# Gate products by token tile instead of a seven-product scheme, and another order of the last products of a down-projection, in a two-layer decoder trunk

## The chip, the cores and the metric

The kernel runs on one core of one Trainium2 chip. The metric is the device time of one execution in microseconds (us). Engines are named as in the profile: PE multiplies matrices, PEld loads its weights, DVE is the vector engine, ACT the scalar engine, POOL the general one, SP issues most of the DMAs.

## The reference

512 tokens, width 1024, two layers, all in float32. Layer 0 mixes tokens by an mLSTM, layer 1 by sliding-window attention over a shared K/V that is computed after layer 0. Each layer ends in the same way, and only this end bears on the change:

```python
x = layer_norm(ALPHA * x + mix, mix_ln_g[i], mix_ln_b[i])
x = layer_norm(ALPHA * x + squared_relu_mlp(x, w_up[i], w_down[i]), mlp_ln_g[i], mlp_ln_b[i])
x = x + sigmoid(x @ w_gate[i] + b_gate[i]) * (p[i] @ w_proj[i])
```

`w_up` is 1024x4096, `w_down` 4096x1024, `w_gate` 1024x1024, `w_proj` 256x1024; `p[i]` is the embedding of the layer, 512x256. Below, "gate" means `x @ w_gate` with what follows it, and "embedding projection" `p @ w_proj`.

## The kernel before

**Number format.** Every float32 operand of a product is split into a high part (ACT, line 76, 133 or 546) and a low part (DVE, line 77, 134 or 547), and a product is three matmuls: high x high, low x high, high x low (`mm3`, lines 88, 89, 90). One "product of 24 matmuls" below is 8 blocks of 128x128 by 512 columns, three matmuls each.

**Tiles of tokens.** The residual is four tiles `res[0..3]` of 128 tokens by 1024. `XH`, `XL` hold the transposed activations, 8 blocks of 128 by 512 tokens, high and low.

**Weights.** `load_w` loads 128x1024 of a weight into `wraw` (three buffers), and splits it into `whi` and `wlo` (six buffers each). SP issues these loads.

**The seven-product scheme (`seven`).** A 512x1024 by 1024x1024 product is done as the seven half-size products M1 to M7 of the Strassen-Winograd scheme, in place of eight. It needs sums of weight blocks (lines 519, 522, 525, 529, on DVE, two each), sums of activation blocks (`S1`, `S23`, `S4A`), and a callback `on` that adds each product into the results it belongs to. The order is M1, M2, M5, M6, M7, M3, M4. The down-projection of an MLP is done so in four quarters of 1024 of the hidden width (`mlp`, q = 0..3), and the gate once per layer (`ple`).

**End of an MLP.** In the last quarter, M3 completes the residual of tiles 0 and 1 and M4 that of tiles 2 and 3. Each is followed by `ln_finish`: statistics (line 142), a power on POOL (138), two passes of DVE over 128x1024 (145, 146), and then `put_seven`, which transposes the tile on PE (565) and writes `XH`/`XL` for tiles 0 and 1, and, once the second of a pair (0,2), (1,3) is there, the activation sums for the gate. The layer norm's gain and bias are loaded by POOL into the two buffers `bc` after M7 has let go of them (lines 670 to 677).

**End of a layer (`ple`).** The embedding projection (16 groups of 3 matmuls; `p` lies in columns of `XH`/`XL` that are not in use) is written before the gate, so its 48 matmuls run right after M4. Then come the seven gate products; as each result is complete, sigmoid (ACT, 723), product with the projection (DVE, 724), addition to the residual (DVE, 725). In layer 0 `done` then transposes the tile (129) into `XH`/`XL` for the K/V projection that follows, whose weights are split on POOL (line 77 with engine POOL) rather than on DVE. In layer 1 the result goes to the output.

**What sets the order.** A list scheduler of the framework orders each engine's instructions once, when the kernel is built, by program order among those that its own estimate says are ready; on the chip each engine runs its list strictly in that order. Each tile is a fixed stretch of on-chip memory, and a tile may be written when the tiles that lay in that stretch before are released. A pool's tiles lie in the order of their first use. `pm` (of `mlp`, tiles `A11h`, `A11l`, `A12h`, `A12l`, `s1`) and `pp` (of `ple`) take turns on one stack: in layer 0 they end at the same byte (145376), in layer 1 they begin at the same byte (184320, where `A11h` lies).

Of the kernel before, what the change touches and what calls it, by code (L numbers as in the profile page):

```python
# [10 lines left out]
F32 = mybir.dt.float32  # L11
# [34 lines left out]
def yoco_kernel(ctx: ExitStack, tc: tile.TileContext, A: dict, out: bass.AP):  # L46
# [90 lines left out]
        V.tensor_scalar(dst, var, EPS, None, ALU.add)  # L137
        GP.tensor_tensor(dst, dst, nhalf[:, :n], ALU.pow)

    def ln_finish(t, st, g, b, put=None):  # L140
        mv = small.tile([P, 2], F32, tag="mv", name="mv")
        V.bn_aggr(mv, st)
        rs = small.tile([P, 1], F32, tag="rs", name="rs")
        rsqrt_eps(rs, mv[:, 1:2], 1)
        V.scalar_tensor_tensor(res[t], res[t], mv[:, 0:1], g, ALU.subtract, ALU.mult)
        V.scalar_tensor_tensor(res[t], res[t], rs, b, ALU.mult, ALU.add)  # L146
        if put is None:
            transpose_in(res[t], t, XH, XL)
            ACT.mul(res[t], res[t], ALPHA)
            if t >= 2:  # L150
                r = res[t - 2][:, 512:]
                V.tensor_sub(r, r, res[t][:, 512:])
        else:
            put(t)

    def add_res(t, half, ps, alpha):
        r = res[t][:, half * 512:(half + 1) * 512]
# [333 lines left out]
    def seven(A_, wsrc, on):  # L491
# [31 lines left out]
        product("S2", ops(r11), "M6")  # L523
        for c in range(2):
            V.tensor_add(r12[c], r12[c], r22[c])
        product("S3", ops(r12), "M7")
        product("S4", ops(r22), "M3")
        for c in range(2):
            V.tensor_add(r21[c], r21[c], r11[c])
        product("A22", ops(r21), "M4")  # L530
# [25 lines left out]
    half0 = {}  # L556

    def put_seven(t):

        a = t % 2  # L560
        raws = []
        for b in range(2):
            pt = tp_bank()
            for j in range(4):
                PE.transpose(pt[:, tsl(j)], res[t][:, tsl(4 * b + j)], ident)
            raw = xr()
            ACT.copy(raw, pt)
            raws.append(raw)
            if t < 2:
                v = raw.rearrange("p (k c) -> p k c", c=P)  # L570
                both_parts((XH[:, 4 * b:4 * b + 4, tsl(t)], XL[:, 4 * b:4 * b + 4, tsl(t)]), v)
        if t < 2:
            half0[t] = raws
            return
        a11, a12 = half0[a]
        a21, a22 = raws
        s1 = xr()
        V.tensor_sub(s1, a21, a22)
        V.tensor_sub(a21, a21, a11)
        V.tensor_sub(a11, a11, s1)  # L580
        V.tensor_sub(a12, a12, a11)
        sl = tsl(a)
        kc = lambda x: x.rearrange("p (k c) -> p k c", c=P)
        both_parts([x[:, :, sl] for x in sp["S1"]], kc(s1))
        both_parts([x[:, 0, :, sl] for x in sp["S23"]], kc(a11))
        both_parts([x[:, 1, :, sl] for x in sp["S23"]], kc(a21))
        both_parts([x[:, 0, :, sl] for x in sp["S4A"]], kc(a12))
        both_parts([x[:, 1, :, sl] for x in sp["S4A"]], kc(a22))

    def mlp(i, side):  # L590
        mctx = ExitStack()
# [5 lines left out]
        for q in range(NQ):  # L597
# [54 lines left out]
            def on(step, a, bank):  # L652
                r0, r1 = res[a], res[2 + a]
                t1, t6, t7 = T1[:, a, :], T6[:, a, :], T7[:, a, :]
                if step == "M1":
                    gather(t1, bank)
                    if last:
                        V.tensor_add(r0[:, lo_], r0[:, lo_], t1)
                elif step == "M2":
                    V.tensor_add(r0[:, lo_], r0[:, lo_], bank)  # L660
                    if last:
                        V.bn_stats(sts[a][:, 0, :], r0[:, lo_])
                elif step == "M5":
                    V.tensor_add(r1[:, hi_], r1[:, hi_], bank)
                    if last:
                        V.tensor_add(r0[:, hi_], r0[:, hi_], r1[:, hi_])
                elif step == "M6":
                    gather(t6, bank)
                    if last:
                        V.tensor_sub(t6, t6, t1)  # L670
                        V.tensor_add(r0[:, hi_], r0[:, hi_], t6)
                elif step == "M7":
                    gather(t7, bank)
                    if last:
                        V.tensor_add(t7, t7, t6)  # L675
                        V.tensor_add(r1[:, hi_], r1[:, hi_], t7)
                        V.tensor_sub(r1[:, lo_], r1[:, lo_], t7)
                        V.bn_stats(sts[2 + a][:, 1, :], r1[:, hi_])
                        if a == 1:
                            gb_[:] = [bcast(A["mlp_ln_g"][i]), bcast(A["mlp_ln_b"][i])]  # L680
                elif step == "M3":
                    V.tensor_add(r0[:, hi_], r0[:, hi_], bank)
                    if last:
                        V.bn_stats(sts[a][:, 1, :], r0[:, hi_])
                        ln_finish(a, sts[a], *gb_, put_seven)
                elif step == "M4":
                    V.tensor_add(r1[:, lo_], r1[:, lo_], bank)
                    if last:
                        V.bn_stats(sts[2 + a][:, 0, :], r1[:, lo_])
                        ln_finish(2 + a, sts[2 + a], *gb_, put_seven)  # L690
# [5 lines left out]
    def ple(i, last, side):  # L696
        plctx = ExitStack()
        pp = pool(f"pp{i}", stack=plctx, side=side, reuse_waits="tile")
        T = sp["T"]
        halves = (slice(0, 512), slice(512, 1024))  # L700
        raw = wpool.tile([P, 1024], F32, tag="raw", name="wraw", bufs=3)
        nc.sync.dma_start(raw, A["pT"][i])
        spare = [x[:, 0:4, 256:512] for x in (XH, XL)]
        both_parts(spare, raw.rearrange("p (j c) -> p j c", c=256))
        bg = bcast(A["ple_b_gate"][i])
        bs = pp.tile([P, 512], F32, name="bs")
        V.tensor_add(bs, bg[:, halves[0]], bg[:, halves[1]])
        pjs = {}
        for half in range(2):
            wph, wpl = load_w(A["w_proj"][i, half], 1024)  # L710
            for t in range(NT):
                pj = mm_bank()
                for k in range(2):
                    j = k * NT + t
                    h, l = (x[:, j // 2, (j % 2) * P:(j % 2 + 1) * P] for x in spare)
                    sl = slice(k * 512, (k + 1) * 512)
                    mm3(pj, h, l, wph[:, sl], wpl[:, sl], k == 0, k == 1)
                pjs[t, half] = pp.tile([P, 512], F32, name=f"pj{t}{half}")
                ACT.copy(pjs[t, half], pj)

        def fin(t, half, s, pj):
            r = res[t][:, halves[half]]
            ACT.activation(s, s, AF.Sigmoid)
            V.tensor_mul(s, s, pj)  # L724
            V.tensor_add(r, r, s)  # L725
            if last:
                nc.sync.dma_start(out[tsl(t), halves[half]], r)

        def stile():
            return xr()  # L730

        keep = {}

        def on(step, a, bank):
            if step == "M1":
                V.tensor_add(T[:, a, :], bank, bg[:, halves[0]])
            elif step == "M2":
                s = stile()
                V.tensor_add(s, T[:, a, :], bank)
                fin(a, 0, s, pjs[a, 0])  # L740
            elif step == "M5":
                s = keep["z", a] = stile()
                V.tensor_add(s, bank, bs)
            elif step == "M6":
                V.tensor_sub(T[:, a, :], bank, T[:, a, :])
                s = keep["c", a] = stile()
                V.tensor_add(s, T[:, a, :], keep["z", a])
            elif step == "M7":
                V.tensor_add(T[:, a, :], T[:, a, :], bank)
                s = keep["z", a]  # L750
                V.tensor_add(s, s, T[:, a, :])
                fin(2 + a, 1, s, pjs[2 + a, 1])
            elif step == "M3":
                s = keep["c", a]
                V.tensor_add(s, s, bank)
                fin(a, 1, s, pjs[a, 1])
                done(a)
            elif step == "M4":
                s = stile()
                V.tensor_sub(s, bank, T[:, a, :])  # L760
                fin(2 + a, 0, s, pjs[2 + a, 0])
                done(2 + a)

        if not last:
            bo = bcast(A["b_b_o"])

        def done(t):
            if last:
                return
            transpose_in(res[t], t, XH, XL)  # L770
            V.scalar_tensor_tensor(res[t], res[t], ALPHA, bo, ALU.mult, ALU.add)
            nc.sync.dma_start(spill[t], res[t])

        at = lambda b: lambda k, a: tuple(p[:, 4 * b + k, tsl(a)] for p in (XH, XL))
        seven(sset((at(0), at(1))), lambda half: [A["w_gate"][i, half, c] for c in range(4)], on)
        plctx.close()

    dpool = ctx.enter_context(tc.tile_pool(name="dpool", bufs=1, space=bass.MemoryType.DRAM))
# [290 lines left out]
```

## Time and profile before

| | |
|---|---|
| median of 3 runs | 1255.28 us (1254.99 to 1256.64) |
| the profiled execution's own time | 1252.41 us |
| its span in the profile | 1250.7 us |
| granted clock of PE, mean | 0.98 |
| PE busy | 1180.0 us, 94% |
| DVE busy | 932.4 us, 75% |
| ACT busy | 612.5 us, 49% |
| POOL busy | 150.2 us, 12% |

Times below are counted from the start of the span. The table of stretches (windows) in the profile gives, for each stretch, the busy time and the count of instructions of each engine, and the clock that PE was granted as a share of full speed. In the timeline the start, the duration and the shape of each instruction stand; matmuls are pipelined, so the distance of two starts and not the duration tells their rate.

### The profile page before, as it was taken

How to read it: one execution, taken by the hardware profiler on the slowest of the kernel's cores; microseconds unless marked ns; L12 is line 12 of the kernel's file. 1: busy time of each engine (PE TensorE's matmuls, PEld its weight loads, DVE VectorE, ACT ScalarE, POOL GpSimd, SP SyncE). 2: the span in 40 equal slices, each digit the busy share in tenths (PEclk: the TensorE clock that was granted, in tenths of full speed). 3: DMA queues.
4: the chain of work that ended last, by engine and by line, in shares of the span. 5: the costliest groups of instructions: out<-in, count | busy, mean ns of one | idle time of the engine just before them, and what ended most of it. 6: DMA issues, size and time to landing. Idle time of an engine off the chain costs nothing.

```text
span 1250.7 us, 15664 instructions
## 1 busy us (share of the span) xinstructions
PE 1180.0 (94%) x5846; PEld 1000.4 (80%) x5846; DVE 932.4 (75%) x1504; ACT 612.5 (49%) x1049; POOL 150.2 (12%) x245
## 2 busy tenths in 40 slices
PE   9999999999999999996879898989999999999868
PEld 8899988888888888885658898779888888888656
DVE  7556567696595784999995788496847858669998
ACT  4544542665454544643533555335645446355453
POOL 1011110000000000002054664310000000000020
PEclk9999999999999999997989999999999999999989
DMA  7222224506225043051052111261350530613201
GB/s 247 88 88 69 84 70 168 202 2 201 68 71 182 17 146 124 20 183 44 27 189 86 61 42 35 75 234 63 91 164 15 159 112 24 203 43 112 90 18 68
DMA packets 35564, 124.55 MB, mean 100 GB/s; under 512 B 4048, under 2 KB 4320, under 8 KB 35488
## 3 DMA queue, kind: packets, MB, share of 16 engines
q1 hardware_dynamic: 33408, 116.46, 29.1%
q0 software_dynamic: 2080, 7.09, 1.7%
q8 instruction: 46, 0.75, 0.2%
q14 instruction: 30, 0.25, 0.1%
HBM read 119.34 MB, written 4.19 MB: 99 GB/s over the span
## 4 chain that ended last, share of the span: by engine, by line
PE 76%; DVE 17%; ACT 3%; issue 3%; DMA 1%; SPq 0%; POOL 0%; DVEq 0%; ACTq 0%; POOLq 0%
PE mm L88 23%; PE mm L89 23%; PE mm L90 23%; DVE wlo L77 3%; ACT whi L76 1%; ACT pr L904 1%; DVE xr L724 1%; DVE QS L873 1%; DVE res L725 1%; DVE smax L890 1%; PE tp L88 1%; DVE res L146 1%; PE tp L89 1%; PE tp L90 1%; DVE sc L889 1%
## 5 line engine op out<-in xcount | busy, mean ns | idle before, releaser
L76 ACT CAST whi<-wraw 128x1024 fp32r<-128x1024 f32 (+1 forms) x160 | 165.1, 1035 | 244.2 <-PE mm L90 141.8
L77 DVE TENSOR_TENSOR wlo<-wraw,whi 128x1024 fp32r<-128x1024 f32 (+1 forms) x144 | 174.7, 1214 | 133.1 <-ACT whi L76 132.4
L89 PE MATMUL mm<-XL,whi 128*128 128x512 f32 (+1 forms) x640 | 235.4, 368 | 0.0
L88 PE MATMUL mm<-XH,whi 128*128 128x512 f32 (+1 forms) x640 | 234.6, 369 | 0.5 <-ACT ot L232 0.3
L90 PE MATMUL mm<-XH,wlo 128*128 128x512 f32 (+1 forms) x640 | 235.1, 368 | 0.0
L76 ACT CAST whi<-rb 128x1024 fp32r<-128x1024 f32 x100 | 104.8, 1050 | 109.6 <-PE mm L89 53.1
L77 DVE TENSOR_TENSOR wlo<-rb,whi 128x1024 fp32r<-128x1024 f32 x100 | 121.3, 1218 | 38.7 <-ACT whi L76 38.7
L88 PEld LDWEIGHTS mm<-XH,whi 128*128 128x128 f32 x640 | 119.9, 188 | 21.1 <-ACT ot L232 0.7
L90 PEld LDWEIGHTS mm<-XH,wlo 128*128 128x128 f32 x640 | 120.5, 188 | 19.9
L89 PEld LDWEIGHTS mm<-XL,whi 128*128 128x128 f32 x640 | 120.6, 188 | 19.7
L88 PE MATMUL mm<-whi,XH 128*128 128x412 f32 (+2 forms) x352 | 121.0, 344 | 4.6 <-DVE q L863 3.2
L90 PE MATMUL mm<-whi,XL 128*128 128x412 f32 (+2 forms) x352 | 120.5, 344 | 0.0
L89 PE MATMUL mm<-wlo,XH 128*128 128x412 f32 (+2 forms) x352 | 120.3, 342 | 0.0
L121 POOL DMA_DIRECT2D bc<-in_mlp_ln_g_dram x2 | 1.2, 580 | 649.6 <-DVE bc L675 649.6
L88 PEld LDWEIGHTS mm<-whi,XH 128*128 128x128 f32 x352 | 67.9, 193 | 9.8 <-DVE q L863 4.1
L89 PEld LDWEIGHTS mm<-wlo,XH 128*128 128x128 f32 x352 | 67.8, 193 | 5.9 <-issue 1.5
L90 PEld LDWEIGHTS mm<-whi,XL 128*128 128x128 f32 x352 | 67.7, 192 | 4.8 <-issue 0.8
L88 PE MATMUL mm<-whi,S23h 128*128 128x512 f32 x160 | 64.6, 404 | 0.0
L89 PE MATMUL mm<-wlo,S23h 128*128 128x512 f32 x160 | 64.5, 403 | 0.0
L88 PE MATMUL mm<-whi,S4Ah 128*128 128x512 f32 x160 | 63.3, 396 | 0.0
L89 PE MATMUL mm<-wlo,S4Ah 128*128 128x512 f32 x160 | 63.3, 396 | 0.0
L90 PE MATMUL mm<-whi,S23l 128*128 128x512 f32 x160 | 63.3, 403 | 0.0
(322 smaller groups left out, 2453.2 us busy)
## 6 DMA issues: line engine op xcount, KB each, us to landing
wraw<-in_w_up_dram SPq DMA_DIRECT2D x64, 512.0 KB, 3.6
rb<-in_w_down_dram SPq DMA_DIRECT2D x48, 512.0 KB, 4.3
wraw<-in_w_down_dram SPq DMA_DIRECT2D x16, 512.0 KB, 3.8
wraw<-in_w_vo_dram SPq DMA_DIRECT2D x19, 412.0 KB, 3.2
rb<-in_w_gate_dram SPq DMA_DIRECT2D x12, 512.0 KB, 3.6
wraw<-in_w_qk_dram SPq DMA_DIRECT2D x8, 512.0 KB, 4.4
wraw<-in_w_out_dram SPq DMA_DIRECT2D x8, 512.0 KB, 3.7
wraw<-in_w_q_dram SPq DMA_DIRECT2D x8, 512.0 KB, 3.6
```

Of the source, the lines that this page charges most:

```text
L76: ACT.copy(hi, raw)
L77: eng.tensor_sub(lo, raw, f32(hi))
L88: PE.matmul(o, lh, rh, start=start, stop=False)
L89: PE.matmul(o, lh, rl, start=False, stop=False)
L90: PE.matmul(o, ll, rh, start=False, stop=stop)
L146: V.scalar_tensor_tensor(res[t], res[t], rs, b, ALU.mult, ALU.add)
L724: V.tensor_mul(s, s, pj)
L725: V.tensor_add(r, r, s)
L873: V.tensor_sub(QS[other, hs, tsl(t)], pv[own], f32(QS)[own, hs, tsl(t)])
L889: V.copy_predicated(cur, mk, prev)
L890: V.tensor_reduce(smax[:, :, pr], cur, AX.X, ALU.max)
L904: ACT.activation(pt_[:, par, pr, :], scs[pr][:, par, :], AF.Exp, scale=ASCALE, bias=nm[:, par, pr:pr + 1], accum_out=sm[:, par, pr:pr + 1])
```

## The change

1. The gate is eight plain groups instead of seven products of sums: for each half of the output columns and each token tile t, one group of 24 matmuls (the four weight blocks of a half stay in `whi`/`wlo` for all four tiles). `put_seven` goes; `ln_finish` transposes straight into `XH`/`XL`. The very last group (layer 1, second half, tile 3) is done in two pieces of 256 columns.
2. All embedding projections are written before the gates; `p` has tiles of its own (`ph`, `pl`, in `pp`), and the results lie in four tiles in the memory of `rb`. Gate weights come through `load_w` only.
3. In `seven`, which only the down-projections use now, the order of the last three products is M3, M7, M4 (before: M7, M3, M4).
4. Gain and bias of the MLP's layer norm are loaded after M2 into the stretches of `A11h` and `A11l`.

```diff
-    def ln_finish(t, st, g, b, put=None):
+    def ln_finish(t, st, g, b, mlp_next=True):
...
-        if put is None:
-            transpose_in(res[t], t, XH, XL)
+        transpose_in(res[t], t, XH, XL)
+        if mlp_next:
             ACT.mul(res[t], res[t], ALPHA)
...
+        product("S4", ops(r22), "M3")
         product("S3", ops(r12), "M7")
-        product("S4", ops(r22), "M3")
         for c in range(2):
             V.tensor_add(r21[c], r21[c], r11[c])
         product("A22", ops(r21), "M4")
...
+                        if a == 1:
+                            for x, n in ("h", "mlp_ln_g"), ("l", "mlp_ln_b"):
+                                v = pm.tile([P, 4, 256], F32R, tag=f"A11{x}", name=f"A11{x}")
+                                v = f32(v).rearrange("p k c -> p (k c)")
+                                nc.gpsimd.dma_start(v, A[n][i].partition_broadcast(P))
+                                gb_.append(v)
...
-                        if a == 1:
-                            gb_[:] = [bcast(A["mlp_ln_g"][i]), bcast(A["mlp_ln_b"][i])]
...
+        ph = pp.tile([P, 2, S], F32R, name="ph")
+        pl = pp.tile([P, 2, S], F32R, name="pl")
         raw = wpool.tile([P, 1024], F32, tag="raw", name="wraw", bufs=3)
         nc.sync.dma_start(raw, A["pT"][i])
...
+        split(raw, 1024, flat(ph), flat(pl))
         bg = bcast(A["ple_b_gate"][i])
...
+        pjs = [sp["s"].tile([P, 1024], F32, tag="rb", name="pj", bufs=6) for _ in range(NT)]
         for half in range(2):
+            hs = slice(half * 512, (half + 1) * 512)
             wph, wpl = load_w(A["w_proj"][i, half], 1024)
             for t in range(NT):
                 pj = mm_bank()
                 for k in range(2):
...
+                    mm3(pj, ph[:, k, tsl(t)], pl[:, k, tsl(t)], wph[:, sl], wpl[:, sl], k == 0, k == 1)
+                ACT.copy(pjs[t][:, hs], pj)
+        for half in range(2):
+            w = [load_w(A["w_gate"][i, half, c], 1024) for c in range(4)]
+            for t in range(NT):
+                ps = mm_bank()
+                s = xr()
+                step = 256 if last and half == 1 and t == NT - 1 else 512
+                for c0 in range(0, 512, step):
...
+                    for k in range(KD):
...
+                        mm3(ps[:, cs], XH[:, k, tsl(t)], XL[:, k, tsl(t)], wh[:, sl], wl[:, sl], k == 0, k == KD - 1)
+                    V.tensor_add(s[:, cs], ps[:, cs], bg[:, rs])
+                    ACT.activation(s[:, cs], s[:, cs], AF.Sigmoid)
+                    V.tensor_mul(s[:, cs], s[:, cs], pjs[t][:, rs])
+                    V.tensor_add(res[t][:, rs], res[t][:, rs], s[:, cs])
+                    if last:
+                        nc.sync.dma_start(out[tsl(t), rs], res[t][:, rs])
+                if last:
+                    continue
+                if half == 1:
+                    transpose_in(res[t], t, XH, XL)
+                    V.scalar_tensor_tensor(res[t], res[t], ALPHA, bo, ALU.mult, ALU.add)
+                    nc.sync.dma_start(spill[t], res[t])
```

More of the change, by code (lines that the diff above doesn't have):

```diff
@@ L152, in ln_finish @@
                 V.tensor_sub(r, r, res[t][:, 512:])
-        else:
-            put(t)
     def add_res(t, half, ps, alpha):
@@ L554, in sset @@
                 "S4": at(sp["S4A"], 0), "A22": at(sp["S4A"], 1)}
[L556 to L588, printed above, removed]
     def mlp(i, side):
@@ L684, in on @@
                         V.bn_stats(sts[a][:, 1, :], r0[:, hi_])
-                        ln_finish(a, sts[a], *gb_, put_seven)
+                        ln_finish(a, sts[a], *gb_, mlp_next=False)
                 elif step == "M4":
@@ L689, in on @@
                         V.bn_stats(sts[2 + a][:, 0, :], r1[:, lo_])
[L690 removed]
+                        ln_finish(2 + a, sts[2 + a], *gb_, mlp_next=False)
             at = lambda pair: lambda k, a: tuple(p[:, k, tsl(a)] for p in pair)
@@ L698, in ple @@
         pp = pool(f"pp{i}", stack=plctx, side=side, reuse_waits="tile")
-        T = sp["T"]
-        halves = (slice(0, 512), slice(512, 1024))
+        ph = pp.tile([P, 2, S], F32R, name="ph")
+        pl = pp.tile([P, 2, S], F32R, name="pl")
         raw = wpool.tile([P, 1024], F32, tag="raw", name="wraw", bufs=3)
         nc.sync.dma_start(raw, A["pT"][i])
-        spare = [x[:, 0:4, 256:512] for x in (XH, XL)]
-        both_parts(spare, raw.rearrange("p (j c) -> p j c", c=256))
+        split(raw, 1024, flat(ph), flat(pl))
         bg = bcast(A["ple_b_gate"][i])
-        bs = pp.tile([P, 512], F32, name="bs")
-        V.tensor_add(bs, bg[:, halves[0]], bg[:, halves[1]])
-        pjs = {}
+        if not last:
+            bo = bcast(A["b_b_o"])
+        pjs = [sp["s"].tile([P, 1024], F32, tag="rb", name="pj", bufs=6) for _ in range(NT)]
         for half in range(2):
+            hs = slice(half * 512, (half + 1) * 512)
             wph, wpl = load_w(A["w_proj"][i, half], 1024)
@@ L713, in ple @@
                 for k in range(2):
-                    j = k * NT + t
-                    h, l = (x[:, j // 2, (j % 2) * P:(j % 2 + 1) * P] for x in spare)
                     sl = slice(k * 512, (k + 1) * 512)
[L717 to L775, printed above, removed]
+                    mm3(pj, ph[:, k, tsl(t)], pl[:, k, tsl(t)], wph[:, sl], wpl[:, sl], k == 0, k == 1)
@@ new lines, in ple @@
+                ACT.copy(pjs[t][:, hs], pj)
[6 more added lines that the diff above has]
+                for c0 in range(0, 512, step):
+                    cs = slice(c0, c0 + step)
+                    rs = slice(half * 512 + c0, half * 512 + c0 + step)
+                    for k in range(KD):
+                        wh, wl = w[k // 2]
+                        sl = slice((k % 2) * 512 + c0, (k % 2) * 512 + c0 + step)
+                        mm3(ps[:, cs], XH[:, k, tsl(t)], XL[:, k, tsl(t)], wh[:, sl], wl[:, sl], k == 0, k == KD - 1)
[11 more added lines that the diff above has]
+                    nc.sync.dma_start(spill[t], res[t])
```

## The prediction

> **What bounds the kernel now.** I read the page first, then the waits of PE around the end of layer 0, then the table of stretches, then DVE's groups in one of them.
>
> ```profile
> span 1250.7 us, 15664 instructions
> PE 1180.0 (94%) x5846; PEld 1000.4 (80%) x5846; DVE 932.4 (75%) x1504; ACT 612.5 (49%) x1049; POOL 150.2 (12%) x245
> ```
>
> PE is busy 94% of the span, so added matmuls cost their full time unless they take the place of idle PE. PE's idle time is 70.7 us, and the change works in the two places where much of it lies. The waits of PE in 505 to 660 us, the end of layer 0's MLP, its gate, and the start of K/V:
>
> ```profile
> PE tp L565 <- DVE mv L142: 11.6, 1, 11.6
> PE tp L129 <- DVE res L725: 8.0, 2, 6.2
> PE mm L88 <- ACT S1h L546: 3.8, 1, 3.8
> ```
>
> One wait of 11.6 us for the layer norm, 3.8 us for the activation sums of the gate, 8.0 us for the gate's last results. The table of stretches puts them in order: M3 with M4 and before it M7 (542.7 to 559.8), the embedding projections (to 570.7), the wait, the gate's first 3.4 us and all of it (586.3 to 633.6), the wait before K/V, the first K/V matmuls; one stretch after the 3.8 us wait; then wait, gate and tail of layer 1; last, layer 0's `w_out`, which is done in plain groups already.
>
> ```profile
> 542.70:559.80 17.10, 17.10 (x75) 13.75 (x74) 16.94 (x23) 6.31 (x6) 0.57 (x1) 1.00 0.64 196
> 559.80:570.70 10.90, 10.90 (x49) 8.69 (x47) 10.90 (x15) 6.01 (x9) 0.53 (x1) 1.00 0.13 48
> 570.70:586.30 15.60, 3.55 (x17) 3.16 (x17) 15.60 (x22) 4.28 (x7) 4.34 (x3) 0.57 0.00 1
> 586.30:589.70 3.40, 3.40 (x16) 2.85 (x15) 3.40 (x6) 1.88 (x4) 2.01 (x3) 0.96 0.10 13
> 586.30:633.60 47.30, 43.45 (x190) 34.69 (x188) 45.87 (x60) 25.14 (x37) 9.79 (x7) 0.96 0.23 67
> 633.60:643.40 9.80, 1.77 (x12) 1.60 (x13) 9.80 (x8) 2.74 (x4) 6.59 (x3) 0.71 0.57 161
> 643.40:646.80 3.40, 3.40 (x10) 2.72 (x9) 3.40 (x2) 2.12 (x5) 3.18 (x11) 0.50 0.00 0
> 606.10:609.50 3.40, 3.40 (x10) 2.74 (x11) 3.40 (x7) 1.85 (x3) 0.00 (x0) 0.64 0.01 2
> 1182.30:1197.80 15.50, 3.44 (x18) 3.03 (x17) 15.50 (x22) 4.11 (x7) 6.21 (x3) 0.67 0.01 1
> 1197.80:1244.50 46.70, 42.86 (x186) 33.97 (x184) 44.81 (x65) 23.16 (x34) 2.22 (x3) 0.96 0.12 42
> 1244.50:1250.70 6.20, 0.00 (x0) 0.00 (x0) 2.67 (x4) 0.63 (x1) 0.00 (x0) 0.84 0.29 108
> 173.00:222.00 49.00, 48.85 (x239) 40.21 (x238) 36.10 (x66) 16.43 (x25) 9.36 (x8) 1.00 0.44 146
> ```
>
> Columns after the length: PE, PEld, DVE, ACT, POOL busy, granted clock, DMA share, GB/s. What to see: from 542.7 on, DVE is busy without a break (16.94 + 10.90 + 15.60 of 43.6 us) while PE runs dry. So it is DVE's work that sets when the gate starts, not a latency. DVE's groups in 542.7 to 586.3:
>
> ```profile
> L77 DVE TENSOR_TENSOR wlo<-wraw,whi 128x1024 fp32r<-128x1024 f32 x6 | 7.3, 1217 | 0.0
> L77 DVE TENSOR_TENSOR wlo<-rb,whi 128x1024 fp32r<-128x1024 f32 x4 | 4.9, 1217 | 0.2 <-ACT whi L76 0.2
> L145 DVE SCALAR_TENSOR_TENSOR res<-res,mv,bc 128x1024 f32<-128x1024 f32 x3 | 3.8, 1276 | 0.0
> L146 DVE SCALAR_TENSOR_TENSOR res<-res,rs,bc 128x1024 f32<-128x1024 f32 x2 | 2.6, 1279 | 0.0
> L525 DVE TENSOR_TENSOR rb<-rb 128x1024 f32<-128x1024 f32 x2 | 2.4, 1218 | 0.0
> L519 DVE TENSOR_TENSOR rb<-rb 128x1024 f32<-128x1024 f32 x2 | 2.4, 1216 | 0.0
> L522 DVE TENSOR_TENSOR rb<-rb 128x1024 f32<-128x1024 f32 x2 | 2.4, 1214 | 0.0
> L529 DVE TENSOR_TENSOR wraw<-wraw,rb 128x1024 f32<-128x1024 f32 x2 | 2.4, 1196 | 0.0
> ```
>
> Eight sums of gate weights (9.6 us) and ten weight splits (12.2 us) stand among the layer norm's passes.
>
> **The change, part by part.** First the prices of a matmul, of eight transposes, and of a DVE instruction:
>
> ```profile
> 629.91 0.39 PE L88 MATMUL mm<-whi,S4Ah 128*128 128x512 f32 x1
> ...
> 632.71 0.40 PE L88 MATMUL mm<-whi,S4Ah 128*128 128x512 f32 x1
> 582.33 1.94 PE L565 MATMUL tp<-ident,res 128*128 128x128 f32 x8 [11.59 <-DVE mv L142]
> 592.92 1.03 PE L565 MATMUL tp<-ident,res 128*128 128x128 f32 x8
> 642.69 1.08 PE L129 MATMUL tp<-ident,res 128*128 128x128 f32 x4 [6.24 <-DVE res L725]
> 559.21 1.22 DVE L519 TENSOR_TENSOR rb<-rb 128x1024 f32<-128x1024 f32 x1
> 560.34 0.68 DVE L682 TENSOR_TENSOR res<-res,mm 128x512 f32<-128x512 f32 x1
> ```
>
> (a) *Plain gates.* Twelve matmuls in 2.80 us, 0.233 each: a group of 24 is 5.6 us. Eight groups instead of seven are +5.6 us a layer, +11.2 us in all, if nothing else moved. The row 173 to 222 shows that plain groups run dense (48.85 of 49.00 us) with DVE at 74%. The half-size pieces at the very end I take at equal cost per column.
>
> (b) *Start of layer 0's gate.* It needs tile 0's layer norm and four gate weights. Of DVE's solid stretch up to 586.3, the eight sums go, and the splits drop from ten to eight (two each for M4 and the projections stay, four gate blocks for six). That is ten instructions; one of 1.22 us holds DVE for 1.13 to 1.14 (559.21 to the next start at 560.34), so 11.4. One of the three L145 passes is tile 2's and can follow (1.2). The low part of `p`, before done into `XL` ahead of this stretch, may now fall into it, since `ph`, `pl` end where `pm` ended and wait for `A12` and `s1` (+1.1). 586.3 - 11.4 - 1.2 + 1.1 = 574.8. The floor is PE: 570.7, plus 2.1 us for two tiles' transposes, 572.8. M3 ahead of M7 and the early gain and bias let DVE take tiles 0 and 1 under M7 and M4, but do not shorten its list. DVE's order is fixed at the build and need not be the best one; I add 3 us: 578, a gain of 8 us. Ends: 573, and 586 where the order wastes all.
>
> (c) *The gate of layer 0 to K/V.* Now 586.3 to 643.4, 57.1 us. After: eight groups 44.8, transposes of tiles 2 and 3 2.1 (the row of 1.03), and of `done` for tiles 0 to 2 3.1, together 50.0. The 3.8 us wait for the sums goes with the sums. The 8.0 us wait goes too: tile 0's result is complete three groups (16.8 us) before the gate ends, and K/V starts with tile 0. It is late next only for tile 3, which K/V reads 16.8 us after the gate's end. K/V start: 578 + 50 = 628 against 643.4, 15.4 earlier. K/V's first matmuls ran at half clock (0.50 in the table), ten in 3.4 us where 14.6 would fit: 1.1 us or more, and four half-tile transposes (2.4 us) stood within K/V of which one tile's (1.0) remains. With 2 us for these, and 0.5 returned for a cold restart of the gate, layer 0 gains about 17. K/V's weights 2 and 3 wait for buffers that the last gate group frees, and POOL needs this long for them, with DVE beside it slowed:
>
> ```profile
> 622.67 2.81 POOL L77 TENSOR_TENSOR wlo<-wraw,whi 128x1024 fp32r<-128x1024 f32 x1 [30.47 <-ACT whi L76]
> 623.16 2.87 DVE L724 TENSOR_TENSOR xr<-xr,pj 128x512 f32<-128x512 f32 x1
> 631.77 0.68 DVE L724 TENSOR_TENSOR xr<-xr,pj 128x512 f32<-128x512 f32 x1
> 1201.80 1.27 DVE L146 SCALAR_TENSOR_TENSOR res<-res,rs,bc 128x1024 f32<-128x1024 f32 x1
> 541.93 0.68 DVE L547 TENSOR_TENSOR S4Al<-xr,S4Ah 128x512 fp32r<-128x512 f32 x1
> 542.80 0.40 PE L88 MATMUL mm<-whi,S23h 128*128 128x512 f32 x1
> ```
>
> A block is free 4.2 and 2.8 us ahead of the gate's end (three and two quarters of 5.6) and needed 2.8 and 4.2 us after it; two splits of 2.8 and two ACT casts fit. A POOL split costs DVE 2.2 us (2.87 against 0.68); in the second half DVE has some 4.6 us of work per group of 5.6 (five passes of 0.68 and one of 1.2), so two such collisions delay late tiles, which have slack. I take nothing, up to 4 us.
>
> (d) *Layer 1.* Here `pp` begins where `pm` began: `ph` lies exactly on the gain, `pl` on the bias. They can't be written before the last layer-norm pass has read these, so the projections no longer cover the layer norm. Before, that last pass ended at 1203.07 (row above). Less the same ten instructions, 1191.7; then `pl`, 1.2: the projections can start at 1193, or 1188 if gate splits follow the norm. The raw `p` also keeps one of three `wraw` buffers all this time, so SP feeds projection and gate weights through two; I count that in the 3 us of order. Queued on ACT behind the waiting `ph` cast are the casts of tiles 2 and 3. PE can fill in with the gate of tile 0, possible from 1197.8 - 12.4 = 1185.4, with the 3 us 1188.4. From there 11.1 (projections) + 44.8 + 2.1 + 0.5 = 58.5: 1246.9. The tail is now 6.2 us, with half-size pieces about 0.9 less (three passes of DVE and one of ACT, some 0.68 each, a third shorter): 1252.2, layer 1 loses 1.5. Ends: gate at 1182, gain 4; projections at 1196 with nothing ahead of them, loss 8.
>
> (e) *M3 ahead of M7.* M3 now starts where M7 did, 542.80, and `S4Al` ended at 542.61: no wait, but no slack; if DVE keeps the splits of M7 ahead, up to 2.4 us, twice. I take zero, DVE's list being re-made for the new order. In the other six down-projections nothing on the path changes: same instructions, and the sums are ready a product ahead. The gain's DMAs wait on POOL for M1 alone; POOL has nothing else there.
>
> **Sum.** -17 + 1.5 = -15.5. The profiled execution, 1252.41, becomes 1236.9. It ran 2.9 us under the median of the runs; the median becomes 1255.28 - 15.5 = 1239.8, I say 1240. About 0.2%, 2.5 us, is what such a measurement can tell from no change.
>
> [...] After the 11.6 us wait the first eight transposes took 1.94 us, later ones 1.03, and the gate's matmuls behind them ran at 0.96 of the clock, 16 in 3.4 us: the transposes had brought the clock up. [...]
>
> **Rivals.** *Layer 1 gains as well* (17%): PE fills the wait with two gate groups and DVE has no lag: layer 0 -21, layer 1 -4, 1230. For it: ten DVE instructions less. Against: two raw buffers.
>
> *DVE's order wastes the saving in layer 0* (16%): the gate starts at 586 as now, only the part behind it gains: -9, with layer 1 at +5: 1251. For it: the passes of the layer norm stand behind sums and splits in DVE's list now, too.
>
> *PE blocks ahead of M4* (8%, the other side): PE's list is fixed, and if tile 0's transposes stand in it ahead of M4, PE waits for DVE in front of M4, then M4's own layer norm starts later. Each us of wait moves all behind it. If tile 0 is ready at 572, PE waits from 554 to 572, M4 ends at 578, the gate starts at 589, and layer 0 gains only about 6; in layer 1 the norm of tiles 2 and 3 ends near 1197, and it loses 10: 1259. It decides from about 16 us of wait in both layers. Against it: now the scheduler put them behind the projections.
>
> *The gates start cold* (4%): the clock does not rise before them, although the wait is short or the transposes stand there, 10 matmuls in 3.4 us as at 606.1: 1242. [...]
>
> **Numbers.** The forecast has 55%, with its own range 1233 to 1247. Ends of the bounds: -21 - 4 and -7 + 8, that is 1230 to 1256; I leave out the blocked case and part of the third: 1229 to 1252. Faster than 1252.8: forecast 0.53, both gain 0.17, cold 0.04, half of the third 0.08: 0.82. Slower: 0.08 and 0.03 of the third: 0.11. Rest 0.07.
>
> **What would show it.** PE's waits: no wait for `S1h`, none for L725 before K/V; K/V's first matmul near 628; a PE wait of 5 to 8 us after the projections in layer 0. Layer 1: the cast of `ph` behind the last L145, projections after or among the first gate groups, last matmul near 1247 before the shift. 192 gate matmuls a layer. It would be wrong if PE stood between M3 and M4, if DVE's stretch stayed solid to 586, or if the projections of layer 1 ran right behind M4.

## The result, and the profile after

The changed kernel takes 1262.53 us (median, 1260.29 to 1263.61) against 1255.88 us (1254.99 to 1256.64) for the kernel before beside it: ratio 1.0051, 95% interval 1.0033 to 1.0068. It is slower by about 6.6 us, or 0.5%, where 15.5 us less were forecast. The profiled execution took 1262.99 us. Its span is 10.6 us longer than that of the profiled one of before; of the difference to 6.6 us, 3.5 come from before's profiled execution, which lay that far under the median of its runs.

The head of the page after:

```profile
span 1261.3 us, 15669 instructions
PE 1196.9 (95%) x5918; PEld 1017.4 (81%) x5918; DVE 869.6 (69%) x1429; ACT 586.7 (47%) x1010; POOL 147.6 (12%) x245
```

PE has 72 instructions more and 16.9 us more of busy time, DVE 62.8 us less. So DVE's work did go, and the time did not follow. PE's longest waits after (us in total, times, longest), around the end of layer 0 (505 to 665 us):

```profile
PE tp L129 <- DVE res L146: 14.9, 3, 10.4
PE mm L88 <- DVE kv L769: 4.1, 1, 4.1
```

and the longest in layer 1 (1100 to 1262 us):

```profile
PE tp L129 <- DVE res L146: 15.3, 4, 10.5
```

The waits for `S1h` and for L725 are gone, as forecast. The wait for the layer norm is not: it was one of 11.6 us, and is now 14.9 us in several pieces. The stretches of after (length, PE, PEld, DVE, ACT, POOL busy, granted clock, DMA share, GB/s) are, in order: M3, M7 and M4; idle; the transposes; the embedding projections; the gate; then idle, transposes, projections, gate and tail of layer 1.

```profile
542.70:560.80 18.10, 18.08 (x78) 14.21 (x76) 17.30 (x27) 5.99 (x6) 0.00 (x0) 1.00 0.38 117
560.80:571.10 10.30, 0.00 (x0) 0.00 (x0) 10.30 (x17) 2.09 (x2) 3.14 (x4) 0.61 0.77 237
571.10:583.80 12.70, 7.61 (x32) 6.12 (x33) 12.66 (x18) 4.86 (x8) 2.90 (x2) 0.50 0.17 56
583.80:596.60 12.80, 12.80 (x50) 10.27 (x50) 2.67 (x4) 5.73 (x10) 0.00 (x0) 0.87 0.21 59
596.60:643.60 47.00, 46.85 (x220) 38.74 (x219) 26.08 (x31) 16.33 (x22) 9.50 (x4) 1.00 0.23 76
1175.60:1186.10 10.50, 0.06 (x1) 0.00 (x0) 10.50 (x18) 2.09 (x2) 3.24 (x3) 0.75 0.57 182
1186.10:1198.80 12.70, 7.68 (x32) 6.17 (x33) 12.67 (x18) 4.91 (x8) 2.91 (x2) 0.50 0.18 58
1198.80:1211.20 12.40, 12.40 (x50) 10.05 (x49) 2.62 (x4) 5.68 (x10) 0.00 (x0) 0.89 0.21 60
1211.20:1256.00 44.80, 44.28 (x217) 37.29 (x216) 19.31 (x27) 9.77 (x13) 0.00 (x0) 1.00 0.14 51
1256.00:1261.30 5.30, 0.02 (x1) 0.00 (x0) 1.28 (x3) 0.42 (x1) 0.00 (x0) 0.83 0.08 26
```

Read the second and the third row. Before, the 10.9 us behind M4 held the embedding projections (10.90 us of PE), while DVE did the layer norm. Now PE does nothing there, and the 12.8 us of projections come after the norm, when DVE has little left to do (2.67 us). The timeline of PE shows the new order, the transposes of all four tiles ahead of the projections:

```profile
560.39 0.39 PE L90 MATMUL mm<-whi,S4Al 128*128 128x512 f32 x1
571.19 1.94 PE L129 MATMUL tp<-ident,res 128*128 128x128 f32 x8 [10.40 <-DVE res L146]
573.52 2.29 PE L129 MATMUL tp<-ident,res 128*128 128x128 f32 x8 [0.39 <-DVE mv L142]
578.50 1.94 PE L129 MATMUL tp<-ident,res 128*128 128x128 f32 x8 [2.69 <-DVE res L146]
582.28 1.94 PE L129 MATMUL tp<-ident,res 128*128 128x128 f32 x8 [1.83 <-DVE res L146]
583.87 0.78 PE L88 MATMUL mm<-whi,ph 128*128 128x512 f32 x1
```

The last matmul of M4 in the kernel before, in layer 0 and in layer 1:

```profile
559.43 0.39 PE L90 MATMUL mm<-whi,S4Al 128*128 128x512 f32 x1
...
1171.08 0.39 PE L90 MATMUL mm<-whi,S4Al 128*128 128x512 f32 x1
```

Before, then, M4 ended at 559.83, the gate started at 586.33 and K/V at 643.43; in layer 1 the times are 1171.46 and 1197.76, and the end 1250.7. The ledger of the two profiled executions is:

- From M4's end to the gate, 26.5 us became 35.8 in layer 0, and 26.3 became 35.6 in layer 1: +9.3 each.
- The gate itself, up to K/V, went from 57.1 to 47.0: -10.1.
- The gate and tail of layer 1 went from 52.9 to 50.1: -2.9.
- K/V has a wait of 4.1 us where there was one of 1.3: +2.8.

That is +8.4. The rest of the 10.6, 2.2 us, lies in the other stretches: 1.0 ahead of M4's end in layer 0, and 1.2 between K/V and M4 of layer 1. Single executions differ by as much there: M4 of layer 0 ended between 559.76 and 562.67 in three executions further down whose edits differ only behind that point.

### The profile page after: what moved, and what is told of

It reads as the page before. It is cut to its first block, busy times and chain, and to the rows that moved or that the text cites. A ratio compares the mean times of both kernels' runs of the same rounds, so it can differ in the third digit from the quotient of the medians.

```text
span 1261.3 us, 15669 instructions
## 1 busy us (share of the span) xinstructions
PE 1196.9 (95%) x5918; PEld 1017.4 (81%) x5918; DVE 869.6 (69%) x1429; ACT 586.7 (47%) x1010; POOL 147.6 (12%) x245
## 4 chain that ended last, share of the span: by engine, by line
PE 84%; DVE 10%; ACT 2%; DMA 2%; issue 2%; POOL 0%; SPq 0%; DVEq 0%; ACTq 0%
PE mm L88 26%; PE mm L89 26%; PE mm L90 26%; DVE wlo L77 1%; PE tp L129 1%; DVE res L146 1%; ACT pr L838 1%; DVE res L145 1%; DVE QS L807 1%; DVE smax L824 1%; PE tp L88 1%; DVE sc L823 1%; PE tp L89 1%; PE tp L90 1%; DMA xraw<-in_xT_dram 1%
## 5 line engine op out<-in xcount | busy, mean ns | idle before, releaser
L88 PE MATMUL mm<-whi,XH 128*128 128x512 f32 (+2 forms) x424 | 147.7, 349 | 7.9 <-DVE kv L769 4.1
L89 PE MATMUL mm<-wlo,XH 128*128 128x512 f32 (+2 forms) x424 | 147.6, 348 | 0.0
L90 PE MATMUL mm<-whi,XL 128*128 128x512 f32 (+2 forms) x424 | 147.3, 348 | 0.0
L76 ACT CAST whi<-rb 128x1024 fp32r<-128x1024 f32 x80 | 84.1, 1051 | 106.5 <-PE mm L89 54.4
L77 DVE TENSOR_TENSOR wlo<-rb,whi 128x1024 fp32r<-128x1024 f32 x80 | 97.4, 1222 | 38.9 <-ACT whi L76 38.9
L88 PEld LDWEIGHTS mm<-whi,XH 128*128 128x128 f32 x424 | 82.0, 193 | 15.9 <-DVE kv L769 4.5
L89 PEld LDWEIGHTS mm<-wlo,XH 128*128 128x128 f32 x424 | 82.0, 194 | 8.2 <-issue 1.5
L90 PEld LDWEIGHTS mm<-whi,XL 128*128 128x128 f32 x424 | 82.0, 194 | 6.9 <-issue 0.8
L129 PE MATMUL tp<-ident,res 128*128 128x128 f32 x160 | 30.2, 339 | 35.8 <-DVE res L146 32.6
L129 PEld LDWEIGHTS tp<-ident,res 128*128 128x128 f32 x160 | 23.5, 175 | 42.4 <-issue 36.7
```

The costliest lines, as they stand in the source:

```text
L76: ACT.copy(hi, raw)
L77: eng.tensor_sub(lo, raw, f32(hi))
L88: PE.matmul(o, lh, rh, start=start, stop=False)
L89: PE.matmul(o, lh, rl, start=False, stop=False)
L90: PE.matmul(o, ll, rh, start=False, stop=stop)
L129: PE.transpose(pt[:, tsl(j)], src[:, tsl(b + j)], ident)
```

## The experiments

Each time stands with its ratio to runs of the kernel before that were taken beside it, and the 95% interval of that ratio.

Theory A: the projections' input `ph`, `pl` lies in the pool `pp`, and nothing of `pp` is put in the engines' lists until the pool `pm`, whose room it takes, has been let go as a whole. Gain and bias now lie in `pm` until the last pass of the layer norm, so the projections stand behind the norm in both layers, whether bytes are shared or not. Rivals: the bytes that `ph` and the gain share (they are the same bytes in layer 1 only); the new order of the products; `ph` and `pl` in `pp` as such.

**`ph`, `pl` elsewhere.** They go into `S1`, free since M5.

```diff
-        pp = pool(f"pp{i}", stack=plctx, side=side, reuse_waits="tile")
-        ph = pp.tile([P, 2, S], F32R, name="ph")
-        pl = pp.tile([P, 2, S], F32R, name="pl")
+        ph, pl = (flat(x).rearrange("p (k c) -> p k c", c=S) for x in sp["S1"])
```

> The changed kernel with ph and pl laid into the two S1 tiles, which are free after M5, instead of into pp. Theory A (the projections lost their place: with ph, pl in a pool that takes pm's stretch, the scheduler holds them until gain and bias are let go, so 48 matmuls stand behind the layer norm instead of under it): projections run right behind M4 in both layers, the gate starts near 575 and 1190 instead of 596.6 and 1211.3, time 1222 us (1214 to 1232). Rival B (the scheduler puts the transposes first because they come earlier in the program, wherever ph lies): as the changed kernel, 1262. Rival C (DVE's list sets the gate's start anyway, the projections only fill a gap that stays): the gate starts no earlier than 587 and 1202, 1245 or more.

Measured: 1232.12 us (1231.52 to 1233.41), ratio to before 0.9816 (0.9802 to 0.9831). PE's two longest waits around layer 0's gate:

```profile
PE tp L129 <- DVE mv L142: 4.8, 1, 4.8
PE mm L88 <- DVE kv L767: 4.3, 1, 4.3
```

The timeline of PE, from the last projection of layer 0 to the start of K/V, then from M4's last matmul to the gate in layer 1 (projections and transposes between them left out):

```profile
570.61 0.40 PE L90 MATMUL mm<-whi,S1l 128*128 128x512 f32 x1
575.77 2.79 PE L129 MATMUL tp<-ident,res 128*128 128x128 f32 x12 [4.76 <-DVE mv L142]
578.22 0.65 PE L88 MATMUL mm<-whi,XH 128*128 128x512 f32 x1
...
628.60 0.47 PE L88 MATMUL mm<-whi,XH 128*128 128x512 f32 x1
...
1157.85 0.40 PE L90 MATMUL mm<-whi,S4Al 128*128 128x512 f32 x1
...
1176.61 0.78 PE L88 MATMUL mm<-whi,XH 128*128 128x512 f32 x1
```

The projections (now reading `S1h`, `S1l`) run right behind M4 and end at 571.0. Of the 10.4 us of idle PE, a wait of 4.8 behind the projections is left. The gate starts at 578.22 and K/V at 628.60. One edit of where 8 KB of each partition lie is worth 30 us. The time is 10 us above what I expected. In both layers the gate starts 18.4 us behind M4's end, against 35.8 and 35.6 in the changed kernel, but I had expected some 21 us less and not 17. The gates also take longer than in the changed kernel, 50.4 against 47.0 us up to K/V and 53.8 against 50.1 in layer 1 with the tail, with 20 of the 32 transposes now within them and not ahead. The wait for `kv` has no part in this: the changed kernel had it as well. Against before, where the gate and tail of layer 1 took 52.9 us, the plain form gains nothing there beyond the earlier start.

**Shared bytes taken away.** An 8 KB tile ahead of `ph` and `pl` in `pp`, so that they lie beside the gain and not on it.

```diff
+        pad = pp.tile([P, 2048], F32, name="pad")
+        V.memset(pad[:, 0:1], 0.0)
         ph = pp.tile([P, 2, S], F32R, name="ph")
```

> The changed kernel with an unused 8 KB tile ahead of ph and pl in pp, so that in layer 1, too, ph and pl share no byte with gain and bias (in layer 0 they share none already). If shared bytes are what holds the projections, layer 1 gains about 20 us: 1242. If the scheduler counts the whole pool pm as one thing when it makes the lists (theory A as the wait in layer 0 suggests, where no byte is shared), the lists stay and the time stays: 1262, at most 2 less as a real wait of layer 1 goes.

Measured: 1261.61 us, ratio 1.0043 (1.0026 to 1.0060). PE's longest wait in layer 0, then in layer 1:

```profile
PE tp L129 <- DVE res L146: 14.9, 3, 10.4
```

```profile
PE tp L129 <- DVE res L146: 15.3, 4, 10.5
```

These are the waits of the changed kernel to the tenth. Shared bytes are not the cause.

**Plain gates alone.** Gain and bias back in `bc` behind M7, and the order M7, M3, M4; `ph`, `pl` stay in `pp`.

```diff
-                        if a == 1:
-                            for x, n in ("h", "mlp_ln_g"), ("l", "mlp_ln_b"):
-                                v = pm.tile([P, 4, 256], F32R, tag=f"A11{x}", name=f"A11{x}")
...
+                        if a == 1:
+                            gb_[:] = [bcast(A["mlp_ln_g"][i]), bcast(A["mlp_ln_b"][i])]
```

> Plain gates alone: the changed kernel with gain and bias loaded into the bc buffers after M7 and the order M7, M3, M4, both as before. Theory A: nothing of pm is held beyond M2, so the projections run behind M4 as before; the gate starts some 10 us earlier than in the kernel before (DVE has ten instructions less), K/V without its wait: 1228 us (1220 to 1240). Rival B: transposes first, 1262 or more.

Measured: 1233.29 us, ratio 0.9822 (0.9807 to 0.9836). So parts 1 and 2 of the change are worth 22.5 us, and `pp` as a place for `ph` and `pl` is harmless when `pm` is let go early.

**Gain and bias early, but elsewhere.** The two rooms exchanged: gain and bias go into `S1` behind M5, `ph` and `pl` stay in `pp`, the new order stays.

```diff
...
-                                v = pm.tile([P, 4, 256], F32R, tag=f"A11{x}", name=f"A11{x}")
...
+                                v = sp["s"].tile([P, 4, 256], F32R, tag=f"S1{x}", name=f"S1{x}", bufs=1)
```

> The changed kernel with the two rooms exchanged: gain and bias of the norm are loaded early as well, behind M5, but into the S1 tiles of the pool ps7, which outlives the projections; the projections' input ph and pl stays in pp, as in the changed kernel, and the order M3, M7, M4 stays. Theory A (pp opens when the last tile of pm is let go, and gain and bias in pm are what keeps pm until the layer norm's end): pm ends with M2's and M1's products, so the 48 projection products run right behind M4 in both layers, gates start within 19 us of M4's end instead of 36, and the time is that of the version with ph and pl in S1: 1232 us (1230 to 1235). Rival (ph and pl in pp are themselves what comes too late): 1255 to 1263 us.

Measured: 1234.6 us (1232.2 to 1235.71), ratio 0.9826 (0.9806 to 0.9847). The stretch from M4's end to the first projection in the changed kernel, and the one from M4's end to just behind the gate's start at 578.85 here:

```profile
560.80:583.90 23.10, 7.71 (x33) 6.22 (x33) 23.03 (x34) 7.05 (x10) 6.04 (x6) 0.55 0.44 137
```

```profile
560.70:579.50 18.80, 14.04 (x62) 11.35 (x60) 18.62 (x30) 8.76 (x14) 5.18 (x6) 0.93 0.59 193
```

Here the 48 projections and the first transposes are done within 18.8 us; in the changed kernel the projections only begin after 23.1. Together with the two runs before this leaves Theory A: an early gain does no harm of this size, `pp` does none either, an early gain in `pm` with the projections' input in `pp` does. What the runs show is that the list depends on which pool holds what. That the scheduler lets go of a pool only as a whole is the reading that fits all four, and no trace shows it by itself.

**The order of the products.** Once with `ph`, `pl` in `S1`, once in the changed kernel:

```diff
-        product("S4", ops(r22), "M3")
         product("S3", ops(r12), "M7")
+        product("S4", ops(r22), "M3")
```

> As e1_proj_free, with the order M7, M3, M4 of the kernel before: what M3 ahead of M7 is worth once the projections cover the layer norm. If DVE's list alone sets the gate's start: within 2 us of e1_proj_free. If tiles 0 and 1 gain from being complete 5.7 us earlier: 6 to 11 us slower than e1_proj_free, over both layers.

Measured, with `ph`, `pl` in `S1`: 1234.99 us, ratio 0.9838 (0.9824 to 0.9853), about 2.9 us more than with the new order, which neither of the two expected outcomes gives. Of this, 1.3 us lie between M4's end and the gate (19.1 and 19.0 us against 18.4 in both layers); where the rest lies is open.

> The changed kernel with the last three products of the down-projections back in the order M7, M3, M4; plain gates, early gain and bias in the last chunk's freed tiles, and the projections' input in the pool pp stay. Theory A (what holds the projections is that pp opens only when pm as a whole is let go, the order of the products is worth little): TensorE still runs the transposes, then the 48 projection products, then the gates in both layers; 1262 to 1266 us. Rival (the order of the products sets off the loss): about 1235 us, as with the projections' input in a tile that is free.

Measured, in the changed kernel: 1256.88 us, ratio 1.0005 (0.9995 to 1.0014). Neither theory had this: the projections do stay behind the norm, and yet 5.6 us come back. The stretch from M4's end to the first projection:

```profile
560.10:580.70 20.60, 6.91 (x30) 5.38 (x29) 20.60 (x31) 7.46 (x10) 6.73 (x4) 0.56 0.39 124
```

DVE is busy for all of the 20.6 us, against 23.03 of 23.10 above. DVE is the bound in both, and the list it has left at M4's end is shorter by 2.4 us. One part of it is that all of M7's additions (lines 645 to 647) lie ahead of M4's end here. DVE's groups in the changed kernel from M4's end to the norm's last pass (560.8 to 582.2; busy, mean ns, idle before) still have two of these, and six low halves of transposed tiles where the old order has four up to its own last pass:

```profile
L134 DVE TENSOR_TENSOR XL<-tp,XH 128x512 fp32r<-128x512 f32 x6 | 4.1, 677 | 0.0
...
L646 DVE TENSOR_TENSOR res<-res,bc 128x512 f32<-128x512 f32 x1 | 0.7, 683 | 0.0
L647 DVE TENSOR_TENSOR res<-res,bc 128x512 f32<-128x512 f32 x1 | 0.7, 681 | 0.0
```

M4's end to the gate is 33.4 and 33.3 us here, against 35.8 and 35.6: the new order costs 2.4 us twice where projections can't cover DVE, and gains some 3 in all where they do.

**The early gain alone,** in the kernel before, with its seven-product gates:

> The kernel before, with one part of the change alone: gain and bias of the norm loaded after M2 into the last chunk's freed tiles A11h and A11l of the pool pm. Gates stay seven products, order stays M7, M3, M4, the projections' input stays in the free half of XH and XL. Theory A (an early gain in pm keeps pm open until the layer norm's last pass, and everything that the next part keeps in pp, here the eight projection results, waits for it): only the products whose results fit the five mm banks run ahead of the transposes (30 of the 48), the other 18 stand behind them in both layers; 18 products at 0.233 us are 4.2 us a layer, so 1258 to 1272 us. Rival (an early gain is worth what a late one costs, and the loss in the changed kernel is only due to ph and pl): at or below before, 1250 to 1256 us.

Measured: 1256.51 us, ratio 1.0004 (0.9994 to 1.0014): above the rival's range and below mine. The list is as Theory A has it: PE stops after 18 and after 30 of the 48 projections, and goes on with the rest behind the transposes.

```profile
569.14 0.79 PE L88 MATMUL mm<-whi,XH 128*128 128x512 f32 x1 [3.52 <-DVE res L691]
...
580.60 3.65 PE L565 MATMUL tp<-ident,res 128*128 128x128 f32 x16 [5.76 <-DVE mv L142]
...
589.78 1.94 PE L565 MATMUL tp<-ident,res 128*128 128x128 f32 x8 [1.15 <-ACT pj L723]
```

The price is not as expected. The gate does start late here, 35.8 us behind M4's end in layer 0 (26.5 before) and 34.6 in layer 1 (26.3), but it then takes 50.3 us up to K/V in place of 57.1, and 45.2 in place of 52.9 in layer 1: all transposes are done ahead of it, and the 3.8 us wait for `S1h` is gone. I had counted the 18 products and not this. Here `pp` holds only the results of the projections, and five banks can wait for it; in the changed kernel it holds their input, and all 48 wait.

**The K/V bias.** With the gate shortened, K/V's second product waits 4.1 us (4.3 with `ph`, `pl` in `S1`) for the bias `kvb`, whose load stands on POOL behind four weight splits and the clearing of the value tiles. First the load goes ahead of the clearing, with that of the query bias `bq` behind it as before; then it goes on SP's queue, while `bq` stays on POOL's:

```diff
+    kvb = pk.tile([P, 512], F32, name="kvb")
+    nc.gpsimd.dma_start(kvb, A["kv_b"].partition_broadcast(P))
...
     for t in range(NT):
         for vv in (vph[t], vpl[t]):
```

> The version with the projections' input in the free tile (1232.1 us), with the loads of the K/V bias and of the query bias issued ahead of the clearing of the value tiles on POOL's queue. There, POOL cleared from 635.8 to 639.3, issued the load at 639.3, and TensorE stood 4.27 us until VectorE had the bias at 643.9. Theory (the 3.5 us of clearing are all that lies between): the load is issued near 635.9, lands near 640.5, TensorE's gap falls to about 1 us, and the time to 1228.5 (1227 to 1230). Rival (the load waits for the memory that the last gate still holds, or clearing after it makes the value tiles late instead): the gap moves or stays, 1231 to 1233 us.

Measured: 1231.74 us, ratio 0.9804 (0.9787 to 0.9821), no gain to speak of, as the rival had it. The issue on POOL (timeline) and the time to landing (DMA issues, last column), first of the version before this edit, then of this one:

```profile
639.27 0.60 POOL L728 DMA_DIRECT2D kvb<-in_kv_b_dram  x1
```

```profile
kvb<-in_kv_b_dram POOLq DMA_DIRECT2D x1, 256.0 KB, 4.6
```

```profile
638.39 0.60 POOL L724 DMA_DIRECT2D kvb<-in_kv_b_dram  x1
```

```profile
kvb<-in_kv_b_dram POOLq DMA_DIRECT2D x1, 256.0 KB, 7.3
```

This execution ran 2.6 us later at this point, so the issue came 3.5 us earlier, which is the length of the clearing. But the load now took 7.3 us, and 2.7 of the 3.5 were lost; PE's gap went from 4.3 to 3.4. A weight load was issued beside it here (at 638.46, on SP), which the version before this edit did not have in that time, while both had a spill. That this traffic is what slowed the load is likely, and no run varies it alone.

```diff
-    nc.gpsimd.dma_start(kvb, A["kv_b"].partition_broadcast(P))
+    nc.sync.dma_start(kvb, A["kv_b"].partition_broadcast(P))
```

> The version with ph and pl in S1 (1232.1 us), with the load of the K/V bias issued from SP's queue instead of POOL's, where it stood behind four weight splits of 3.0 us each and 3.5 us of clearing. Theory (the bias is late only because of POOL's queue): it is issued when the memory of pk is free, near 634, lands at 639 to 641, TensorE's gap of 4.27 us at the second K/V product falls below 1 us, 1228 to 1230 us. Rival (SP's own queue, with the loads of the query weights and the spills behind it, or the shared DMA traffic gives the time back, as putting the load ahead of the clearing did: 4.6 us to landing became 7.3): 1231 to 1233 us.

Measured: 1227.87 us (1227.03 to 1229.67), ratio 0.9773 (0.9752 to 0.9794), the fastest version here, 28 us under before. SP issues the load while POOL still splits (its four splits end at 638.8), and PE's wait for `kv` is gone. The issue on SP, then the one wait that PE has left in 505 to 665 us:

```profile
636.37 0.50 SPq L728 DMA_DIRECT2D kvb<-in_kv_b_dram  x1
```

```profile
PE tp L129 <- DVE mv L142: 4.8, 1, 4.8
```

## Why the prediction was wrong

**(b) and (d), the cover of the layer norm: the step that failed.** Of layer 0 the prediction said that "`ph`, `pl` end where `pm` ended and wait for `A12` and `s1`", and put the floor at the projections' end, 570.7. That took the wait to be one for bytes. In layer 0 the gain lies at other bytes, and still `ph` was cast only behind the last pass that reads the gain (it ends at 580.21). The timeline of DVE and then of ACT in the changed kernel:

```profile
578.93 1.28 DVE L145 SCALAR_TENSOR_TENSOR res<-res,mv,A11h 128x1024 f32<-128x1024 f32 x1
...
582.65 1.22 DVE L77 TENSOR_TENSOR pl<-wraw,ph 128x1024 fp32r<-128x1024 f32 x1
```

```profile
579.63 0.59 ACT L133 CAST XH<-tp 128x512 fp32r<-128x512 f32 x1 [3.19 <-PE tp L129]
...
580.96 1.05 ACT L76 CAST ph<-wraw 128x1024 fp32r<-128x1024 f32 x1
```

The load of the raw `p` was issued at 490.94 and took some 3.5 us, and ACT stood idle for 3.19 us up to 579.63, waiting for a transpose: whatever else the cast waited for, its place in ACT's list held it up to there. So the lists had the projections behind the norm in layer 0 too, and PE's list had the transposes of all four tiles ahead of them. "It needs tile 0's layer norm" was true of the data and not of the list: the gate waited for the norm of all four tiles. It started at 596.6 instead of 578, 18.6 us late, which is the larger part of the miss even though the gate then took 3 us less than reckoned. Of layer 1 the prediction saw the hold, and priced it at 1.5 us since "PE can fill in with the gate of tile 0". PE filled in with nothing: its list was transposes, then projections, then gates. The run with the 8 KB tile ahead, with no shared byte in layer 1 and the same waits, shows that the bytes named there were not the reason either. The gate began 35.6 us after M4's end, where 17 were reckoned for tile 0's gate with the projections behind it.

**(b), DVE's list, right, with some luck.** With the projections free the gate starts at 578.22; 578 was forecast. Three us of that were a guess for DVE's order with no row behind it, so that it agrees to 0.2 us is luck.

**(c) right, but for one queue.** With the projections free, gate to K/V took 50.4 us (forecast 50.0), and K/V started at 628.60 (628). "I take nothing, up to 4 us" for K/V's supply was the wrong end: 4.1 to 4.3 us were lost, not by the splits reckoned there but by the load of the bias behind them. POOL's queue was followed for the weights only. No run shows the 0.5 us that the sums of both layers take for a cold restart of the gate: the gates of the changed kernel ran at 1.00 (596.60 to 643.60 and 1211.20 to 1256.00), and with the projections free the full clock came 0.4 and 2.7 us behind the gate's first product (last section).

**(a) right.** The gates ran dense: 46.85 of 47.00 us of PE, with `done` inside. The tail took 5.30 us, as reckoned in (d).

**(e) mis-sized.** M3 ahead of M7 made PE wait for nothing (18.08 of 18.10 us busy), as said. It was taken at zero and cost 5.6 us, through DVE's list at the end, because nothing covered that list. That this is near the "up to 2.4 us, twice" of (e) is chance: those were a wait of PE at M3's start, which did not come. Where the projections cover DVE's list, the new order is the better one.

**Rivals.** None was this one. The nearest on the slower side, PE blocked ahead of M4, has no trace: PE never stood there. "The gates start cold" came true in part, for the projections: the clock was at half for 3.2 us behind the first of them in layer 0, which cost about 1.5 us (last section). That "layer 1 gains as well" is what the version with the projections free did, with M4's end to the gate going from 26.3 to 18.4 us in layer 1. Of the signs of being wrong, none says what happened; the nearest is DVE's solid stretch, which went on to 583.9, and held the norm of all four tiles by then.

## What to carry to other kernels

Before a buffer is put into memory that "is free by now", ask which allocation group keeps it alive and what opens only when that whole group is let go: here 8 KB per partition of gain and bias in the wrong pool cost 30 us, and PE's waits named only the layer norm (`res`, `mv`), not the room. Work that is meant to cover a wait has to be ready before that wait, by the room of its inputs as well as by their data. Look for it in the list of the engine that would wait, in order of time. When a stage gets shorter, follow the small loads (a bias) through their queue, and not only the large ones.

## What the runs showed of the hardware

The rows below (length, PE, PEld, DVE, ACT, POOL busy, granted clock, DMA share, GB/s) show the granted clock of PE around the first products behind a wait. First the changed kernel around its first projection, which starts at 583.87, behind eight transposes from 582.28:

```profile
582.20:584.00 1.80, 1.72 (x9) 1.75 (x9) 1.66 (x2) 0.58 (x1) 0.00 (x0) 0.50 0.02 5
584.00:586.00 2.00, 2.00 (x7) 1.61 (x6) 1.38 (x2) 0.59 (x1) 0.00 (x0) 0.50 0.46 100
586.00:588.00 2.00, 2.00 (x8) 1.53 (x8) 0.00 (x0) 0.00 (x0) 0.00 (x0) 0.74 0.40 162
588.00:590.00 2.00, 2.00 (x10) 1.63 (x9) 0.00 (x0) 0.79 (x2) 0.00 (x0) 1.00 0.00 0
```

Then the version with `ph`, `pl` in `S1`, in layer 0 (12 unbroken transposes from 575.77, first product at 578.22) and in layer 1 (first product at 1176.61):

```profile
575.70:578.20 2.50, 2.43 (x12) 2.46 (x13) 2.50 (x7) 1.04 (x2) 1.02 (x1) 0.50 0.44 180
578.20:580.20 2.00, 1.70 (x7) 0.83 (x6) 2.00 (x5) 0.72 (x2) 1.68 (x2) 0.90 0.00 0
580.20:582.20 2.00, 2.00 (x11) 1.73 (x12) 2.00 (x3) 0.59 (x1) 0.00 (x0) 1.00 0.00 0
```

```profile
1175.91:1179.32 3.41, 3.41 (x13) 2.47 (x13) 3.41 (x6) 1.17 (x2) 2.37 (x2) 0.50 0.00 0
1179.33:1182.74 3.41, 3.41 (x17) 2.83 (x16) 3.33 (x4) 0.59 (x1) 0.00 (x0) 1.00 0.00 0
```

With one step from 0.50 to 1.00 taken in each place, these rows put the full clock 3.2 us behind the first projection in the changed kernel, and 0.4 and 2.7 us behind the gate's first product in layers 0 and 1 of the other version. These times are estimates from the mean clocks of the rows. In the first case eight transposes right ahead had not brought it; what set the moment, no run varies by itself. The late clock cost the changed kernel about 1.5 us in layer 0: ten projection products took 3.86 us from the first to the eleventh start, where ten at 0.233 take 2.33.

A load of 256 KB landed after 4.6 us, after 7.3 when it was issued 3.5 us earlier on the same queue, beside a weight load, and after 5.3 from SP's queue. Being 3.5 us earlier on the queue was worth 0.8 us on arrival.
